# Retention in small steps inside the attention, block-diagonal states, and VectorE sums in the norm and the down tail

## The chip, the cores and the metric

One Trainium2 chip, one of its cores. The metric is the device time of one execution in microseconds (us), the median over runs. A profiled execution of the same kernel gives the trace. TensorE is PE in the rows (PEld is its weight load), VectorE is DVE, ScalarE is ACT, GpSimd is POOL, SyncE is SP.

## The reference, cut to what matters

Two layers of a trunk over 9 tiles of 128 tokens: tiles 0 to 7 are latent tokens, tile 8 is context. Each layer is

```python
h = rmsnorm(x, norm[0]) * (1.0 + sc1) + sh1
x = x + g1 * rmsnorm(mixer(h), norm[1])      # retention, Fourier, attention, Hyena; one output projection
h = rmsnorm(x, norm[2]) * (1.0 + sc2) + sh2
f = (silu(h @ w_gate) * (h @ w_up)) @ w_down
x = x + g2 * rmsnorm(f, norm[3])
```

The retention has 4 heads of 64, chunks of 128 tokens, and runs forward and backward:

```python
scores = einsum(qc, kc) * dmask              # within a chunk
inner = einsum(scores, vc)
kv = einsum(kc * zeta, vc)                   # a chunk's own 64x64 state
S_next = g_chunk * S + kv_j                  # scan over chunks
cross = einsum(qc * xi, S_prev)
o = inner + cross                            # then a norm over each head, and a gate
```

Beside it stands softmax attention with 4 heads over 9 blocks of keys for the latent tiles.

## The kernel before, in words

All of it is float32. A large product splits each operand into two float32r parts and takes three matmuls (`mm3`, L129 to L131); small products are plain float32, which the trace shows as two passes for each matmul. A scheduler puts each engine's instructions into an order from the order of the source, priorities and its own estimate of durations; at run time each engine follows its order and waits where it must. All layers run one after the other in five stages.

- `phase1`: the first norm, the input projection (`acc`), the Hyena filters and convolution. In layer 0 `norm_mod` (L306) makes each tile `x0`: a VectorE multiply (L313), a sum (L157, helper `tt`) on the engine its argument names, GpSimd by default, then `norm_turn` (L318), eight transposes into `pstr` (L324) and a split into `Th` and `Tl`.
- `phase2`: Fourier, retention and attention. `ret_rope` rotates q and k on VectorE, `ret_tables` makes the decay tables, `ret_states` makes each chunk's state (`rkz` on VectorE, `pskv` on PE at L1062, copies into `Sall`) and scans it with a multiply into `rst` and a sum (VectorE). These three stand ahead of the attention, with a raised priority. `attention` works through 20 pairs of head and query tiles: scores `sc`, softmax, transposes of the probabilities (`pstr`, L918 and L923), products `po`. After each pair it calls `beside`, which takes one step of the retention: a whole `ret_tile` or one part of `ret_group`, 15 steps in all. `ret_tile` transposes q and k (L1088), makes the scores from 64-row halves (L1100), then for each head `inner` from `rsT` (L1107) and two cross products, 64 rows by 64 columns, from `rqx` and `Sall` (L1110).
- `phase3`: the output projection (`wo`) and the second norm. `gate_up`: the SwiGLU products (`gu`).
- `ffn`: the down product into `dq`, three groups of three tiles. `finish` (L1517) ends a tile: its norm, x + y, the next layer's norm through `norm_mod`, and in layer 0 the eight transposes of the tile (`y4`) into `Th`. The two sums of a tile are on GpSimd for tiles up to `ET` (7 in layer 0; in layer 1, which has one sum only, up to 1), otherwise on VectorE.

Of the kernel before, what the change touches and what calls it, by code (L numbers as in the profile page):

```python
# [99 lines left out]
class Kern:  # L100
# [549 lines left out]
    def phase1(self, l):  # L650
        nc, tc, A = self.nc, self.tc, self.A
        with ExitStack() as c:
# [7 lines left out]
            if l == 0:  # L660
# [285 lines left out]
    def attention(self, l, pool, hd, psp, beside):  # L946
# [6 lines left out]
        for n in range(len(pairs) + 2):  # L953
# [24 lines left out]
    def ret_tables(self, l, pool, Sall):  # L978
# [33 lines left out]
        scratch = Sall[:, 4:8].rearrange("p t a b c -> p (t a b c)").rearrange("p (n c) -> p n c", c=P)  # L1012
# [15 lines left out]
    def ret_rope(self, l, keep):  # L1028

        nc = self.nc  # L1030
        tabs = keep.tile([P, 2, 8, 64], F32, name="ropeR")
        nc.sync.dma_start(tabs, self.A["ropeR"])
        Sall = keep.tile([P, 8, 2, 2, 64], F32, name="Sall")
        self.qk = keep.tile([P, NT, 512], F32, name="rqk")
        for t in range(NT):
            if t % 3 == 0:
                nc.sync.dma_start(self.qk[:, t:t + 3], self.proj[l][:, t:t + 3, 256:768])
            if t < CTX:
                tmp = Sall[:, 2 * (t % 2):2 * (t % 2) + 2].rearrange("p a b c d -> p (a b c) d")
                self.rope("v", self.qk[:, t].rearrange("p (h d) -> p h d", h=8), tabs[:, :, t], tmp, 8, 64)  # L1040
        return Sall

    def ret_states(self, l, zt, gt, Sall, keep, psp):

        nc, A = self.nc, self.A
        kvc = keep.tile([P, 2, 2, 64], F32, name="kvc")
        kzs = keep.tile([P, 2, 2, 4, 64], F32, name="rkz", tag="ropeR")
        for d in range(2):
            nc.sync.dma_start(Sall[:, 7 * d, :, d], A["sret"][l, :, :, d])
        for t in range(NT):  # L1050
            if t % 3 == 0:
                v3 = keep.tile([P, 3, 256], F32, name="rv")
                nc.sync.dma_start(v3, self.proj[l][:, t:t + 3, 768:1024])
# [10 lines left out]
            for hh in range(2):  # L1064
                q = slice(64 * hh, 64 * hh + 64)
                if t == CTX:
                    nc.scalar.activation(kvc[q], ps[q, :, :, q], AF.Copy)
                    continue
                for d, dst in ((0, t + 1), (1, t - 1)):
                    if 0 <= dst < 8:  # L1070
                        nc.scalar.activation(Sall[q, dst, :, d], ps[q, :, d, q], AF.Copy)

        nc.sync.dma_start(A["o_st"][l], kvc)
        for d, order in ((0, range(1, 8)), (1, range(6, -1, -1))):
            for t in order:
                prev = t - 1 if d == 0 else t + 1
                tmp = keep.tile([P, 2, 64], F32, name="rst")
                self.tt("v", tmp, Sall[:, prev, :, d], gt[:, :, d:d + 1].broadcast_to([P, 2, 64]), ALU.mult)
                self.tt("v", Sall[:, t, :, d], Sall[:, t, :, d], tmp, ALU.add)

    def ret_tile(self, l, t, vg, o, Dm, xi, Sall, pool, psp):
# [7 lines left out]
        qkT = pool.tile([P, 4, P], F32, name="rqkT")  # L1089
# [12 lines left out]
        for e in range(2):  # L1102
            q = slice(64 * e, 64 * e + 64)
            pi = psp.tile([P, 2, 64], F32, name="psr", tag="r")
            for pr in range(2):
                h = 2 * pr + e
                nc.tensor.matmul(pi[:, pr], sT[:, h], vg[:, 64 * h:64 * h + 64], start=True, stop=not lat)  # L1107
                if lat:
                    for d in range(2):
                        nc.tensor.matmul(pi[:, pr], qx[q, pr, d], Sall[q, t, pr, d], start=False, stop=d == 1)  # L1110
            nc.scalar.activation(o[:, e::2], pi, AF.Copy)

    def ret_group(self, l, g, Dm, xi, Sall, pool, psp):

        nc = self.nc
        vg = pool.tile([P, 3, 512], F32, name="rvg")
        o = pool.tile([P, 12, 64], F32, name="ro", bufs=1)
        for j in range(3):
            self.ret_tile(l, 3 * g + j, vg[:, j], o[:, 4 * j:4 * j + 4], Dm, xi, Sall, pool, psp)
            yield  # L1120
# [19 lines left out]
        for j in range(3):  # L1140
# [3 lines left out]
            rt = pool.tile([P, 2, P], F32, name="rot", bufs=4)  # L1144
# [61 lines left out]
    def phase2(self, l):  # L1206
        nc, tc, A = self.nc, self.tc, self.A
        with ExitStack() as c:
# [11 lines left out]
            steps = (0 for g in range(3) for _ in self.ret_group(l, g, Dm, xi, Sall, rp, psp))  # L1220
# [252 lines left out]
    ET = (7, 1)  # L1473

    def ffn(self, l):
        nc, tc, A = self.nc, self.tc, self.A
        last = l == L - 1
        with ExitStack() as c:
# [38 lines left out]
            def finish(t, ps):  # L1517
# [6 lines left out]
                e = "v" if t > self.ET[l] else "g"  # L1524
                cut = [slice(512 * h, 512 * h + 512) for h in range(2)] if last and t > 6 else [slice(0, D)]
                for q in cut:
                    self.stt(y[:, q], ps[:, q], r[:, 0:1], rows[0][:, q], ALU.mult, ALU.mult)
                    self.tt(e, x[:, q], x[:, q], y[:, q], ALU.add)
                    nc.sync.dma_start(self.xd[l + 1][t][:, q], x[:, q])
                if not last:  # L1530
# [3 lines left out]
                    self.norm_mod(t, x, y, rows[1], rows[2], dn, "tr", None, e)  # L1534
                if t + 3 < NT:
                    load_x(t + 3)

            if not last:
# [7 lines left out]
            for g in range(3):  # L1546
                ps = [dn.tile([P, D], F32, name="dq", tag=f"q{j}") for j in range(3)]
                for f0, n in self.BLOCKS:
                    for j in range(3):
# [4 lines left out]
                        for f in range(f0, f0 + n):  # L1554
                            wh_, wl_, hh, hl = W[NF * g + f]
                            q = slice(j * P, j * P + P)
                            for hs in (slice(0, 512), slice(512, 1024)):
                                self.mm3(ps[j][:, hs], hh[:, q], hl[:, q], wh_[:, hs], wl_[:, hs], f == 0, f == NF - 1)
                        if f0 + n == NF:
                            finish(3 * g + j, ps[j])  # L1560
                    if g == 0 and f0 == 9:
                        load_rows(0)
                        for t in range(3):
                            load_x(t)

# [127 lines left out]
```

## Time and profile before

| | us |
|---|---|
| three runs | 3442.18, 3446.04, 3451.61 |
| median | 3446.04 |
| profiled execution, its own time | 3440.22 |
| its span in the trace | 3438.4 |
| layer 0: attention with retention | about 587 to 833 |
| layer 1: attention with retention | about 2283 to 2520 |
| layer 0: down product | about 1509 to 1813 |

The span is the time from the first to the last instruction. The trace has for each engine when an instruction ran and what it waited for, and for TensorE the granted clock: 1.00 is 2.4 GHz, and a stretch at 0.90 had a fifth of its time at 1.2 GHz. A busy PE is not PE at its peak, since matmuls overlap and their ends are modelled; how far apart matmuls start tells what they cost.

### The profile page before, as it was taken

The page shows a single profiled execution, that of the slowest core. Times are in us where ns is not written, and L with a number is a line of the kernel's source. Part 1 is how long each engine was busy: PE and PEld are TensorE (multiplying, and loading weights), DVE is VectorE, ACT ScalarE, POOL GpSimd, SP SyncE. Part 2 cuts the span into 40 slices and gives each one's busy share as a digit, 9 for nine tenths or more (in the row PEclk, how much of TensorE's full clock was granted, in tenths as well). Part 3 has the DMA queues.
Part 4 walks back from the last instruction along what each step waited for, and adds up shares of the span by engine and source line. Part 5 has one row for each costly group of instructions (what it writes and reads, how often), then busy time and mean ns, then how long its engine had stood idle before and what let it go on. Part 6 is the DMA issues. An engine that isn't in the chain of part 4 may idle for free.

```text
span 3438.4 us, 52711 instructions
## 1 busy us (share of the span) xinstructions
PE 3178.2 (92%) x19198; PEld 2827.2 (82%) x19198; DVE 2361.8 (69%) x4784; ACT 1321.3 (38%) x2510; POOL 665.6 (19%) x611
## 2 busy tenths in 40 slices
PE   7899888999979999989998999899997999998998
PEld 5768777888779999977777788798886999998887
DVE  6676887767788888855547638676767866665454
ACT  3223213555644444433333232254557322223332
POOL 2111110000055555511111011100101422220000
PEclk8899999889999999999999999998898999999999
DMA  6454555114334343365544444541052322225564
GB/s 215 127 170 133 155 163 183 45 28 136 136 93 126 114 128 111 104 203 173 186 151 138 136 132 149 163 117 34 23 162 99 100 72 77 77 65 174 182 206 137
DMA packets 350995, 440.48 MB, mean 128 GB/s; under 512 B 71530, under 2 KB 281703, under 8 KB 350224
## 3 DMA queue, kind: packets, MB, share of 16 engines
q1 hardware_dynamic: 288960, 380.15, 35.6%
q10 hardware_dynamic: 61776, 56.97, 5.4%
q8 instruction: 151, 2.47, 0.3%
q14 instruction: 108, 0.88, 0.1%
HBM read 345.01 MB, written 92.00 MB: 127 GB/s over the span
## 4 chain that ended last, share of the span: by engine, by line
PE 39%; DVE 8%; DMA 3%; ACT 3%; issue 3%; POOL 1%; SPq 0%; ACTq 0%; DVEq 0%; POOLq 0%
PE dq L129 4%; PE dq L131 4%; PE dq L130 4%; PE gu L131 4%; PE gu L129 4%; PE gu L130 4%; PE acc L131 2%; PE acc L130 2%; PE acc L129 2%; DMA wn<-in_win 1%; DVE rq_w L146 1%; PE psr L1110 1%; PE pstr L918 1%; DVE dw L125 1%; ACT y L302 1%
## 5 line engine op out<-in xcount | busy, mean ns | idle before, releaser
L129 PE MATMUL dq<-dw 128*128 128x512 f32 x792 | 312.9, 395 | 13.0 <-ACT dw L120 10.0
L130 PE MATMUL dq<-dw 128*128 128x512 f32 x792 | 312.4, 394 | 0.0
L131 PE MATMUL dq<-dw 128*128 128x512 f32 x792 | 311.0, 394 | 0.2 <-DVE dw L125 0.2
L129 PE MATMUL gu<-X,fw 128*128 128x256 f32 x1024 | 286.0, 282 | 3.7 <-DVE u L157 1.7
L160 DVE SCALAR_TENSOR_TENSOR adacc<-adw,csilu,adacc 128x256 f32<-128x256 f32 x392 | 231.9, 617 | 80.0 <-DMA adw<-in_wada 78.0
L131 PE MATMUL gu<-X,fw 128*128 128x256 f32 x1024 | 283.0, 279 | 3.6 <-DVE fw L125 3.6
L130 PE MATMUL gu<-X,fw 128*128 128x256 f32 x1024 | 282.9, 279 | 0.0
L130 PE MATMUL acc<-wlo,Th 128*128 128x256 f32 (+1 forms) x720 | 213.7, 297 | 6.5 <-DVE wlo L125 6.3
L125 DVE TENSOR_TENSOR dw<-dhr,dw 128x384 fp32r<-128x384 f32 x132 | 74.6, 569 | 208.9 <-ACT dw L120 208.8
L129 PE MATMUL acc<-whi,Th 128*128 128x256 f32 (+1 forms) x720 | 215.4, 301 | 2.2 <-ACT whi L120 1.5
L131 PE MATMUL acc<-whi,Tl 128*128 128x256 f32 (+1 forms) x720 | 215.0, 299 | 0.0
L129 PEld LDWEIGHTS gu<-X,fw 128*128 128x128 f32 x1024 | 192.7, 189 | 14.8 <-issue 7.0
L131 PEld LDWEIGHTS gu<-X,fw 128*128 128x128 f32 x1024 | 192.5, 189 | 4.0 <-DVE fw L125 4.0
L130 PEld LDWEIGHTS gu<-X,fw 128*128 128x128 f32 x1024 | 192.9, 189 | 0.0
L129 PEld LDWEIGHTS dq<-dw 128*128 128x128 f32 x792 | 151.1, 191 | 46.9 <-ACT dw L120 11.1
L129 PE MATMUL gu<-x1s,fw 128*128 128x320 f32 x576 | 180.2, 313 | 6.4 <-DVE u L157 6.4
L157 POOL TENSOR_TENSOR adacc<-adacc,adp 128x256 f32<-128x256 f32 x168 | 152.0, 905 | 157.6 <-ACT adp L272 153.9
L125 DVE TENSOR_TENSOR dw<-dwr,dw 128x1024 fp32r<-128x1024 f32 x132 | 161.4, 1225 | 29.8 <-ACT dw L120 29.4
L131 PE MATMUL gu<-x1s,fw 128*128 128x320 f32 x576 | 180.5, 313 | 1.2 <-DVE fw L125 1.2
L130 PE MATMUL gu<-x1s,fw 128*128 128x320 f32 x576 | 179.8, 312 | 0.0
L131 PEld LDWEIGHTS dq<-dw 128*128 128x128 f32 x792 | 150.9, 191 | 32.9 <-DVE dw L125 1.3
L130 PEld LDWEIGHTS dq<-dw 128*128 128x128 f32 x792 | 151.1, 191 | 31.3
(495 smaller groups left out, 9344.5 us busy)
## 6 DMA issues: line engine op xcount, KB each, us to landing
dwr<-in_wf SPq DMA_DIRECT2D x132, 512.0 KB
adw<-in_wada SPq DMA_DIRECT2D x320, 128.0 KB
dhr<-h SPq DMA_DIRECT2D x132, 192.0 KB
h<-U SPq DMA_DIRECT2D x176, 128.0 KB
X<-in_wf SPq DMA_DIRECT2D x42, 512.0 KB
fr<-in_wf SPq DMA_DIRECT2D x40, 512.0 KB
pj<-pst ACTq DMA_DIRECT2D x90, 128.0 KB
G<-gt SPq DMA_DIRECT2D x36, 256.0 KB
```

The source lines that it names most:

```text
L125: (nc.vector if elo == "dve" else nc.gpsimd).tensor_tensor(out=lo, in0=src, in1=hi, op=ALU.subtract)
L129: mm(ps, lh, rh, start=start, stop=False)
L130: mm(ps, lh, rl, start=False, stop=False)
L131: mm(ps, ll, rh, start=False, stop=stop)
L146: nc.vector.scalar_tensor_tensor(out=w, in0=a, scalar=a[:, 0:1], in1=v, op0=ALU.mult, op1=ALU.mult)
L157: (self.nc.vector if e == "v" else self.nc.gpsimd).tensor_tensor(out=out, in0=a, in1=b, op=op)
L160: self.nc.vector.scalar_tensor_tensor(out=out, in0=a, scalar=s, in1=b, op0=op0, op1=op1)
L302: nc.scalar.activation(junk, x, AF.Square, accum_out=ss)
L918: T(pst[:, j], pr[i][:, (k0 + j) * P:(k0 + j + 1) * P], self.ident)
L1110: nc.tensor.matmul(pi[:, pr], qx[q, pr, d], Sall[q, t, pr, d], start=False, stop=d == 1)
```

## The change

Four things change.

- **Norm.** In layer 0 the nine sums of the first norm go from GpSimd to VectorE.
- **Down tail.** All sums of `finish` go to VectorE. In layer 0 the transposes of a finished tile are no longer issued in `finish`, but later: when two tiles are pending, or in the next group at its second block.
- **States.** `Sall` holds for each pair of heads a 128x128 block with the two 64x64 states on its diagonal and zeros beside them (two GpSimd memsets). A latent tile's cross products are then four matmuls of 128 rows by 128 columns, where there were eight of 64 by 64. The scan is one VectorE instruction for each pair of heads (`stt`, 128x128), two for each step, where it was a multiply and a sum.
- **Weaving.** `ret_states` and `ret_group` become one generator, `retention`, with a pause after each chunk's state, each direction of the scan and each third of a `ret_tile`: 44 steps. `beside` is also called between scores and transposes, up to 64 times. `ret_rope` and `ret_tables` stay where they were; the rotation's scratch moves out of `Sall`. Some tiles share buffers: `rv` with `rvg`, `kvc` with `rqkT`; `rot` has two buffers in place of four.

```diff
-                    self.norm_mod(t, xt[t], xt[t], rw[:, 0], rw[:, 1], psp, "tr", rs[t])
+                    self.norm_mod(t, xt[t], xt[t], rw[:, 0], rw[:, 1], psp, "tr", rs[t], "v")
...
                     probs[n].append(self.att_scores(score[i], ops[h], pool, psp))
+                beside(n)
                 if i < len(turn):
...
+        for hh in range(2):
+            nc.gpsimd.memset(Sall[64 * hh:64 * hh + 64, :, :, :, 64 - 64 * hh:P - 64 * hh], 0.0)
...
-                        nc.scalar.activation(Sall[q, dst, :, d], ps[q, :, d, q], AF.Copy)
+                        nc.scalar.activation(Sall[q, dst, :, d, q], ps[q, :, d, q], AF.Copy)
+            yield
...
-                tmp = keep.tile([P, 2, 64], F32, name="rst")
-                self.tt("v", tmp, Sall[:, prev, :, d], gt[:, :, d:d + 1].broadcast_to([P, 2, 64]), ALU.mult)
-                self.tt("v", Sall[:, t, :, d], Sall[:, t, :, d], tmp, ALU.add)
+                for k in range(2):
+                    self.stt(Sall[:, t, k, d], Sall[:, prev, k, d], gt[:, k, d:d + 1], Sall[:, t, k, d], ALU.mult, ALU.add)
+            yield
+
+    def retention(self, l, tabs, Sall, keep, pool, psp):
+
+        zt, gt, Dm, xi = tabs
+        yield from self.ret_states(l, zt, gt, Sall, keep, pool, psp)
+        for g in range(3):
+            yield from self.ret_group(l, g, Dm, xi, Sall, pool, psp)
...
-        for e in range(2):
-            q = slice(64 * e, 64 * e + 64)
-            pi = psp.tile([P, 2, 64], F32, name="psr", tag="r")
-            for pr in range(2):
-                h = 2 * pr + e
-                nc.tensor.matmul(pi[:, pr], sT[:, h], vg[:, 64 * h:64 * h + 64], start=True, stop=not lat)
-                if lat:
-                    for d in range(2):
-                        nc.tensor.matmul(pi[:, pr], qx[q, pr, d], Sall[q, t, pr, d], start=False, stop=d == 1)
-            nc.scalar.activation(o[:, e::2], pi, AF.Copy)
+        yield
+
+        pi = psp.tile([P, 4, 64], F32, name="psr", tag="r")
+        for pr in range(2):
+            both = pi[:, 2 * pr:2 * pr + 2].rearrange("p h e -> p (h e)")
+            if lat:
+                nc.tensor.matmul(both, qx[:, pr, 0], Sall[:, t, pr, 0], start=True, stop=False)
+            for h in (2 * pr, 2 * pr + 1):
+                nc.tensor.matmul(pi[:, h], sT[:, h], vg[:, 64 * h:64 * h + 64], start=not lat, stop=not lat)
+            if lat:
+                nc.tensor.matmul(both, qx[:, pr, 1], Sall[:, t, pr, 1], start=False, stop=True)
+        nc.scalar.activation(o, pi, AF.Copy)
+        yield
...
-            rt = pool.tile([P, 2, P], F32, name="rot", bufs=4)
+            rt = pool.tile([P, 2, P], F32, name="rot")
...
-                zt, gt, Dm, xi = self.ret_tables(l, rk, Sall)
-                self.ret_states(l, zt, gt, Sall, rk, psp)
+                tabs = self.ret_tables(l, rk, Sall)
...
-                e = "v" if t > self.ET[l] else "g"
...
-                    self.tt(e, x[:, q], x[:, q], y[:, q], ALU.add)
+                    self.tt("v", x[:, q], x[:, q], y[:, q], ALU.add)
...
-                    self.norm_mod(t, x, y, rows[1], rows[2], dn, "tr", None, e)
+                    self.norm_mod(t, x, y, rows[1], rows[2], None, None, None, "v")
+                    late.append((t, y))
...
+                        if len(late) > 1 or late and f0 == 3:
+                            self.norm_turn(*late.pop(0), dn, "tr")
                         if f0 + n == NF:
                             finish(3 * g + j, ps[j])
```

What the scheduler makes of it on TensorE at two places.

The first is the down product of layer 0, at the end of its first group. `dq_16282` before and `dq_16224` after are the third tile's sums, `dq_17014` and `dq_16928` the first sums of the next group, `y4_16796` and `y4_16738` the first tile's finished rows. Before:

```order
L130 MATMUL dq_16282<-dw_16758 128x512
L324 MATMUL pstr_16832<-ident_66,y4_16796 128x128 x4
L324 MATMUL pstr_16839<-ident_66,y4_16796 128x128 x4
L131 MATMUL dq_16282<-dw_16758 128x512
L129 MATMUL dq_17014<-dw_16767 128x512
```

After:

```order
L131 MATMUL dq_16224<-dw_16700 128x512
L129 MATMUL dq_16928<-dw_16709 128x512
...
L129 MATMUL dq_16928<-dw_16780 128x512
L324 MATMUL pstr_16878<-ident_66,y4_16738 128x128 x4
L324 MATMUL pstr_16885<-ident_66,y4_16738 128x128 x4
```

From the end of the first tile to its transposes there were 47 matmuls of 512 columns, and there are 55.

The second is a latent tile of the retention inside the attention of layer 0, its last third (`psr`), with the scores (`sc`) and transposes (`pstr`) of the attention around it. Before:

```order
L918 MATMUL pstr_6066<-ident_66,pr_5904 128x128 x4
L1107 MATMUL psr_6022<-rvg_6001,rsT_6013 128x64
L1110 MATMUL psr_6022<-Sall_5435,rqx_6011 128x64 x2
...
L935 MATMUL po_6111<-pth_5901,vhl_5740 128x256
...
L1110 MATMUL psr_6030<-Sall_5435,rqx_6011 128x64 x2
L129 MATMUL sc_6075<-at_Tl0_5697,at_Th0_5696 128x384
```

After:

```order
L1114 MATMUL psr_6278<-rqkT_6245 128x128 x2
L129 MATMUL sc_6289<-at_Tl1_5765,at_Th1_5764 128x384
...
L131 MATMUL sc_6299<-at_Tl1_5765,at_Th1_5764 128x384
L1122 MATMUL psr_6306<-Sall_5473,rqx_6247 128x128
L1124 MATMUL psr_6306<-rvg_6118,rsT_6276 128x64 x2
L1126 MATMUL psr_6306<-Sall_5473,rqx_6247 128x128
...
L918 MATMUL pstr_6316<-ident_66,pr_6188 128x128 x4
```

Twelve matmuls have become eight, no 64-row matmul stands among them, and nine score matmuls stand between the tile's second third (L1114) and its last.

## Rows read from the trace of the kernel before

**Rows 1.** The page: its span.
```profile
span 3438.4 us, 52711 instructions
```

**Rows 2.** Stretches: length, busy PE, PEld, DVE, ACT, POOL; granted clock, DMA share, GB/s.
```profile
625.00:795.00 170.00, 162.24 (x1041) 144.82 (x1040) 116.01 (x340) 88.97 (x181) 17.55 (x13) 0.90 0.13 34
795.00:833.00 38.00, 32.01 (x225) 28.34 (x224) 34.76 (x89) 26.75 (x49) 1.47 (x1) 1.00 0.47 155
2310.00:2500.00 190.00, 179.61 (x1143) 161.84 (x1142) 130.78 (x387) 99.11 (x200) 19.00 (x14) 0.88 0.15 41
1589.00:1650.00 61.00, 52.80 (x221) 42.63 (x220) 39.52 (x86) 23.77 (x38) 16.90 (x6) 0.89 0.57 184
1695.00:1756.00 61.00, 51.40 (x223) 41.55 (x222) 39.33 (x86) 23.67 (x38) 16.79 (x6) 0.94 0.58 189
1801.00:1850.00 49.00, 42.27 (x225) 35.51 (x224) 35.07 (x79) 14.81 (x32) 10.24 (x4) 0.93 0.55 171
```

**Rows 3.** Timeline of PE over the last third of one latent retention tile.
```profile
635.83 0.43 PE L1107 MATMUL psr<-rvg,rsT 128*128 128x64 f32 x2
636.20 0.66 PE L1110 MATMUL psr<-Sall,rqx 64*128 64x64 f32 x4
...
637.73 0.39 PE L935 MATMUL po<-pth,vhl 128*128 128x256 f32 x1
637.96 0.33 PE L1107 MATMUL psr<-rvg,rsT 128*128 128x64 f32 x2
...
639.75 0.47 PE L129 MATMUL sc<-at_Tl,at_Th 96*128 96x384 f32 x1
```

**Rows 4.** Instructions of L1110 and L1100, and a run of full-height passes on PE.
```profile
L1110 PE MATMUL psr<-Sall,rqx x256: 272/272/473, 636.2 to 2465.9; 64*128 64x64 f32 x128
2295.81 2.02 PE L1062 MATMUL pskv<-rv,rkz 128*128 128x128 f32 x16
631.01 0.72 PE L1100 MATMUL psr<-rqkT 64*128 64x128 f32 x8
```

**Rows 5.** Waits of PE from 590 to 830: total us, times, longest.
```profile
PE pskv L1062 <- DMA rv<-pj: 4.4, 2, 3.8
```

**Rows 6.** Waits of PE from 1580 to 1860.
```profile
PE pstr L324 <- POOL y L157: 20.4, 7, 4.5
```

**Rows 7.** Timelines of POOL and VectorE in and behind that tail.
```profile
1601.36 3.27 POOL L157 TENSOR_TENSOR y<-y,r 128x1024 f32<-128x1024 f32 x1 [4.91 <-issue]
1602.35 2.30 DVE L146 SCALAR_TENSOR_TENSOR rq_w<-rq_u,ss 128x1 f32<-128x1 f32 x1
1607.93 0.21 DVE L146 SCALAR_TENSOR_TENSOR rq_w<-rs,ss 128x1 f32<-128x1 f32 x1
1832.59 1.22 DVE L157 TENSOR_TENSOR x<-x,y 128x1024 f32<-128x1024 f32 x1
```

**Rows 8.** Waits of PE from 40 to 180, and VectorE's timeline there.
```profile
PE pstr L324 <- POOL x0a L157: 4.3, 2, 3.8
PE pstr L324 <- POOL x0c L157: 4.1, 2, 2.2
PE pstr L324 <- POOL x0b L157: 3.0, 2, 1.6
53.69 2.90 DVE L125 TENSOR_TENSOR wlo<-wraw,whi 128x576 fp32r<-128x576 f32 x1
58.74 0.74 DVE L125 TENSOR_TENSOR wlo<-wraw,whi 128x576 fp32r<-128x576 f32 x1
```

**Rows 9.** VectorE's work for the states, both layers: ns least, median, most.
```profile
L157 DVE TENSOR_TENSOR rkz<-rqk,rzt x36: 407/421/442, 589.6 to 2304.4; 128x256 f32<-128x256 f32 x36
L157 DVE TENSOR_TENSOR rst<-Sall,rgt x28: 273/282/1149, 589.4 to 2319.4; 128x128 f32<-128x128 f32 x28
L157 DVE TENSOR_TENSOR Sall<-Sall,rst x28: 272/281/293, 594.2 to 2319.9; 128x128 f32<-128x128 f32 x28
```

**Rows 10.** The chain that ended last: the landing of a 128 KB transfer like `rot`'s.
```profile
2199.39 3.05 DMA mixH<-hyt
```

More of the change, by code (lines that the diff above doesn't have):

```diff
@@ L1011, in ret_tables @@
         nc.scalar.activation(gt, lt, AF.Exp, scale=float(P))
-        scratch = Sall[:, 4:8].rearrange("p t a b c -> p (t a b c)").rearrange("p (n c) -> p n c", c=P)
+        scratch = Sall[:, 4:6].rearrange("p t a b c -> p (t a b) c")
         dist, tm, prow = scratch[:, 0:4], scratch[:, 4:6], scratch[:, 6:8]
@@ L1032, in ret_rope @@
         nc.sync.dma_start(tabs, self.A["ropeR"])
-        Sall = keep.tile([P, 8, 2, 2, 64], F32, name="Sall")
         self.qk = keep.tile([P, NT, 512], F32, name="rqk")
+        part = [keep.tile([P, 8, 64], F32, name="rtmp", tag=tg) for tg in ("rD", "rxi")]
         for t in range(NT):
@@ L1038, in ret_rope, with ret_states @@
             if t < CTX:
[L1039 to L1043, printed above, removed]
+                self.rope("v", self.qk[:, t].rearrange("p (h d) -> p h d", h=8), tabs[:, :, t], part[t % 2], 8, 64)
+        return keep.tile([P, 8, 2, 2, P], F32, name="Sall")
+    def ret_states(self, l, zt, gt, Sall, keep, pool, psp):
         nc, A = self.nc, self.A
-        kvc = keep.tile([P, 2, 2, 64], F32, name="kvc")
+        kvc = pool.tile([P, 4, P], F32, name="kvc", tag="rqkT")[:, 0:2].rearrange("p a (b e) -> p a b e", b=2)
         kzs = keep.tile([P, 2, 2, 4, 64], F32, name="rkz", tag="ropeR")
+        for hh in range(2):
+            nc.gpsimd.memset(Sall[64 * hh:64 * hh + 64, :, :, :, 64 - 64 * hh:P - 64 * hh], 0.0)
         for d in range(2):
-            nc.sync.dma_start(Sall[:, 7 * d, :, d], A["sret"][l, :, :, d])
+            for hh in range(2):
+                q = slice(64 * hh, 64 * hh + 64)
+                nc.sync.dma_start(Sall[q, 7 * d, :, d, q], A["sret"][l, q, :, d])
         for t in range(NT):
             if t % 3 == 0:
-                v3 = keep.tile([P, 3, 256], F32, name="rv")
+                v3 = pool.tile([P, 3, 512], F32, name="rv", tag="rvg")[:, :, 0:256]
                 nc.sync.dma_start(v3, self.proj[l][:, t:t + 3, 768:1024])
@@ L1088, in ret_tile @@
             nc.tensor.transpose(ps[:, j], self.qk[:, t, j * P:j * P + P], self.ident)
-        qkT = pool.tile([P, 4, P], F32, name="rqkT")
+        qkT = pool.tile([P, 4, P], F32, name="rqkT", tag="rqkT")
         nc.scalar.activation(qkT, ps, AF.Copy)
@@ L1101, in ret_tile @@
             nc.vector.tensor_tensor(out=sT[:, e::2], in0=pe[e], in1=Dm[:, e::2], op=ALU.mult)
[L1102 to L1111 removed]
+        yield
[9 more added lines that the diff above has]
+        nc.scalar.activation(o, pi, AF.Copy)
+        yield
     def ret_group(self, l, g, Dm, xi, Sall, pool, psp):
         nc = self.nc
[L1116 removed]
+        vg = pool.tile([P, 3, 512], F32, name="rvg", tag="rvg")
         o = pool.tile([P, 12, 64], F32, name="ro", bufs=1)
         for j in range(3):
[L1119 to L1120 removed]
+            yield from self.ret_tile(l, 3 * g + j, vg[:, j], o[:, 4 * j:4 * j + 4], Dm, xi, Sall, pool, psp)
         st = self.sm.tile([P, 12], F32, name="rmu")
@@ L1215, in phase2 @@
                 Sall = self.ret_rope(l, rk)
-                zt, gt, Dm, xi = self.ret_tables(l, rk, Sall)
-                self.ret_states(l, zt, gt, Sall, rk, psp)
+                tabs = self.ret_tables(l, rk, Sall)
             at = c.enter_context(tc.tile_pool(name="at", bufs=2, reuse_waits="tile", side="right"))
             hd = c.enter_context(tc.tile_pool(name="hd", bufs=1, reuse_waits="tile", side="right"))
-            steps = (0 for g in range(3) for _ in self.ret_group(l, g, Dm, xi, Sall, rp, psp))
+            steps = self.retention(l, tabs, Sall, rk, rp, psp)
             self.attention(l, at, hd, psp, lambda n: next(steps, None))
@@ L1533, in finish @@
                             getattr(self, f"T{nm}")[t // 3] = self.tp.tile([P, 8, 384], F32R, name=f"T{nm}{t // 3}")
-                    self.norm_mod(t, x, y, rows[1], rows[2], dn, "tr", None, e)
+                    self.norm_mod(t, x, y, rows[1], rows[2], None, None, None, "v")
+                    late.append((t, y))
                 if t + 3 < NT:
                     load_x(t + 3)
+            late = []
             if not last:
@@ L1564, in ffn @@
                             load_x(t)
+            for x in late:
+                self.norm_turn(*x, dn, "tr")
     def run(self):
```

1 line of the change is left out of this document (removed).

## The prediction

> **What bounds the kernel now.** I read the page first, then the stretches with their granted clock, then who waits for whom in the places that the diff touches, then the timelines there. The span is 3438.4 us [rows 1]; the execution took 3440.22, which is 5.8 below the median of the runs, so the sum below is made against 3440.2 and a measured median may lie a few us above its result. TensorE is the engine that the others feed. In the attention with retention it is busy for 162.24 of 170 us in layer 0 and 179.61 of 190 in layer 1, while VectorE has 116.01 and 130.78 [rows 2]: there the reader is to see an engine without room, so what leaves its queue shortens the stretch. The same rows show the second thing, the granted clock: 0.90 and 0.88 in these two stretches, where retention tiles stand between the attention's matmuls, and 1.00 in the 38 us behind them, where the attention is alone. At 0.90 the lost tenth of 170 us is 17 us; at 0.88 it is 22.8 us of 190. In the down tail of layer 0 and in its first norm TensorE does wait, and for GpSimd: 20.4 us in 7 waits for `y` [rows 6], and 4.3, 4.1 and 3.0 us for the tiles `x0` [rows 8].
>
> **The change part by part.**
>
> *States merged.* A latent tile's last third ran from 635.83 to 639.75, with one foreign `po` from 637.73 to 637.96 in it, so 3.92 - 0.23 = 3.69 us [rows 3]. In it are 8 passes of L1107 and 16 of L1110: the profile counts 256 of L1110 for 16 latent tiles [rows 4]. Four passes of L1110 take 0.66 us to the end of the last. The new third has 4 matmuls of 128x64 and 4 of 128x128, 16 passes, all on the full height. Sixteen full-height passes with 128 columns took 2.02 us [rows 4]. That saves 1.67 us for a tile, 26.7 us for 16. It is TensorE's own time in a stretch where TensorE has no room, so I take all of it; the zero halves cost nothing more, since the 2.02 us is for 128 columns already. Bounds: 20 us if a quarter of it was cover for late operands, 30 if passes at the lower clock are spared too.
>
> The Trainium skill, page "TensorE: Matmul & The Clock Gate", Part 3 on packing small matmuls, speaks against this: matmuls that use less than the full height and lie in different row groups of the array run side by side. The trace agrees for L1100, where eight 64-row passes took 0.72 us [rows 4], but not for L1110, whose neighbours use the same half and took 0.66 us for four [rows 3].
>
> *Scan and states.* The scan was 28 multiplies and 28 sums at 0.282 and 0.281 us, both layers; it becomes 56 instructions on the same 128x128, the nearest price being these rows, so nothing changes there. The 36 `rkz` at 0.421 us stay [rows 9]. What moves is their place: with `pskv` they stood ahead of the attention in layer 0, and TensorE waited 4.4 us there for the loads `rv` [rows 5]. Woven in, attention stands between them; I take 4 us. The price if this cover is gone is VectorE's time: (36 x 0.421 + 56 x 0.28) = 31 us for both layers, as a bound on the loss. The four loads of `sret` for two, each half as high, are issued on SyncE ahead of `rv`, when nothing waits. The memsets clear 2048 elements twice on 64 partitions; GpSimd's sum of 1024 took 3.27 us [rows 7], so at most some 6.5 us each, 13 us for a layer, on an engine that is busy for 17.55 of 170 us [rows 2]; I take nothing, and the bound upwards is that VectorE is held up for as long.
>
> *Weaving.* Each third of a tile now has attention between its steps, so that the copy of `rqkT` on ScalarE or the mask on VectorE is done when TensorE comes back. The order shows nine score matmuls there. The stretches give the room: 17 + 22.8 = 39.8 us of lost clock, which rows tie to the stretches that hold retention tiles, though not all of that is retention. I take half, 20 us, bounds nothing and 40.
>
> *`rot` with two buffers.* ScalarE's third copy of a group waits until the first transfer has landed. A transfer of this size took 3.05 us [rows 10]; some 2 us of other copies and issues stand between. I take 1 us for each of six groups as a loss, 6 us, bounds nothing and 12. Behind that copy wait the softmax's exponentials, and behind these the transposes.
>
> *Down tail.* Each latent tile has two sums on GpSimd at up to 3.27 us; on VectorE one took 1.22 [rows 7]. While GpSimd held its sum, a 128x1 instruction of VectorE took 2.30 us where it otherwise takes 0.21 [rows 7]. So the chain of a tile becomes shorter by 2 x (3.27 - 1.22) = 4.1 us and by the 2.1 us of one or two such hold-ups, and the order puts 55 in place of 47 matmuls before the transposes. The longest wait was 4.5 us [rows 6], so nearly all 20.4 us go; tile 6, behind which no down product follows, keeps some. I take 17. The three stretches ran at 0.89, 0.94 and 0.93 [rows 2], which is 6.7 + 3.7 + 3.4 = 13.8 us of lost clock; with the waits gone I take half, 7 us, bounds nothing and 13.8. What is late next: VectorE, which gets two sums of 1.22 us for each tile. It was busy for 39.52 of 61 us there [rows 2] with the hold-ups in it. In layer 1 two sums leave GpSimd; nothing of TensorE waits for them: nothing.
>
> *First norm.* The three waits are 11.4 us [rows 8]. But VectorE is busy there nearly without a break, and gets nine sums of 1.22 us, 11 us; what it gets back are hold-ups such as a split of 2.90 us where the next took 0.74 [rows 8]. Chains get shorter, throughput hardly. I take 5 us, bounds a loss of 10 and a gain of 11.4.
>
> **The sum.** 26.7 + 4 + 20 - 6 + 17 + 7 + 5 = 73.7 us. 3440.2 - 73.7 = 3366.5, say **3366 us**.
>
> **The rivals.**
>
> 1. *The clock does not come back.* The dips may belong to the attention itself with its many transposes. For it: layer 1 has the lower clock with the same work. Against it: 1.00 where the attention is alone [rows 2]. The 20 + 7 us fall away: 3366 + 27 = 3393.
> 2. *The attention's own chain bounds.* With retention cheaper, TensorE may wait for ScalarE and VectorE: in the 38 us with attention alone VectorE is busy for 34.76 and TensorE for 32.01 [rows 2]. Against it: that stretch also prepares the next weights. Half of 26.7 + 4 + 20 is lost: 3366 + 25 = 3391.
> 3. *VectorE becomes the bound wherever work was put on it* (slower). In the attention the 31 us of `rkz` and scan come out from their cover and count in full, and the gains of merging, states and clock vanish behind them; in the norm the nine sums are 10 us of loss. It decides once VectorE has under a tenth of its time free, as in those 38 us. Only the tail's 24 us stay: 3440.2 - 24 + 31 + 10 = 3457. Against it: 116.01 of 170 and 130.78 of 190 leave 54 and 59 us [rows 2].
> 4. *Merging saves no passes.* If half-height passes overlapped, 26.7 us would not be there, 3366 + 27 = 3393. The 0.66 us for four of them [rows 3] speaks against it. This is what the packing rule of the page "TensorE: Matmul & The Clock Gate" in the Trainium skill would make of it.
>
> **How the numbers follow.** My forecast has 0.57, rival 1 has 0.24, rival 2 0.10, rival 3 0.06, rival 4 0.03. The predicted time is the forecast's. Downwards the range takes in the whole lost clock (+20 and +7 us) and the norm's 11.4: 3366 - 33 = 3333, and with the upper bound of merging and no loss by `rot` 3324; I set 3325. Upwards it takes in rivals 1, 2 and 4 with the full price of `rot` and half the bound of the memsets: 3393 + 6 + 13 = 3412, set to 3415. Rival 3 stays outside. Changes of under 0.3%, about 10 us, can't be told from none. Rival 3's 3457 lies past that bound on the slow side, and with smaller prices within it: slower 0.04. All other cases are faster by more, but for 0.03 in which prices add up against me: faster 0.93, same 0.03.
>
> **What would show it.** Right: L1110's 64-row passes gone, and a tile's last third at about 2 us; a granted clock of 0.94 or more over the attention with retention, and both stretches shorter by 20 to 35 us; no wait of `pstr` for GpSimd in the tail, and its stretches at 0.95 or more. Wrong: TensorE waiting in the attention for `pr`, `pl` or `ptl` of VectorE in sum for more than 20 us, VectorE busy for nine tenths there, or new waits of the first `acc` products for `wlo` in the norm. The prediction as a whole is wrong if the attention with retention still takes 225 us or more in both layers.

## The result, and the profile after

The changed kernel takes 3422.32 us (median of 4 runs, 3419.45 to 3426.29) against 3448.18 us for the kernel before, measured beside it: a ratio of 0.992, with a 95% interval from 0.9896 to 0.9945. That is faster by 26 us. The forecast was 74 us less, and its range ended at 3415 us, so the time lies outside it. Two thirds of the expected gain are missing, and the question is where they went.

The span on the changed kernel's page, which answers to [rows 1]:

```profile
span 3417.7 us, 52431 instructions
```

Its stretches, with the columns of [rows 2]. The first four rows are the attention with retention of the two layers, each cut in two; the last two are the down tail of layer 0.

```profile
617.00:657.00 40.00, 22.70 (x137) 20.04 (x136) 37.78 (x125) 19.26 (x40) 0.00 (x0) 0.79 0.53 161
660.00:826.00 166.00, 153.73 (x1127) 142.30 (x1125) 136.91 (x415) 105.69 (x220) 22.93 (x16) 0.97 0.22 67
2276.00:2318.00 42.00, 23.82 (x139) 20.40 (x137) 37.29 (x124) 17.50 (x39) 0.00 (x0) 0.76 0.43 135
2320.00:2487.00 167.00, 155.18 (x1131) 142.45 (x1130) 137.84 (x419) 106.35 (x222) 22.91 (x16) 0.97 0.22 67
1616.00:1677.00 61.00, 60.43 (x277) 49.65 (x278) 41.77 (x77) 24.68 (x38) 0.00 (x0) 1.00 0.70 226
1780.00:1830.00 50.00, 44.71 (x237) 38.19 (x236) 32.05 (x81) 16.46 (x33) 0.00 (x0) 0.97 0.52 171
```

Three things are to be seen. The bulk of each attention now runs at 0.97, where [rows 2] had 0.90 and 0.88, so the clock did come back. The tail runs at 1.00, where it had 0.89 and 0.93. But at the head of each attention there is something new: 40 us in which TensorE is busy for 23, and VectorE for 38.

The timeline of TensorE over one latent tile's last third, which [rows 3] showed at 3.69 us, now reads:

```profile
695.60 0.39 PE L1122 MATMUL psr<-Sall,rqx 128*128 128x128 f32 x2
695.82 0.56 PE L1124 MATMUL psr<-rvg,rsT 128*128 128x64 f32 x4
696.21 0.44 PE L1126 MATMUL psr<-Sall,rqx 128*128 128x128 f32 x2
...
697.10 0.44 PE L1126 MATMUL psr<-Sall,rqx 128*128 128x128 f32 x2
```

That is 697.54 - 695.60 = 1.94 us, as forecast ("about 2 us"). So the merged states do what they should. The waits at the head of the attention (total us, times, longest): TensorE's in layer 0 and in layer 1, and SyncE's queue in layer 0:

```profile
PE pstr L918 <- DVE rt L992: 15.1, 1, 15.1
...
PE pstr L918 <- DVE rt L992: 16.6, 1, 16.6
...
SPq L1033 <- DMA pj<-pst: 23.9, 2, 13.0
```

(`rt` is a small instruction of the decay tables, which VectorE ends right behind the first split `pl`.) VectorE's timeline in layer 0 tells what it does meanwhile:

```profile
617.66 0.56 DVE L904 TENSOR_SCALAR_CACHE_REDUCE pr<-sc 128x384 f32<-128x384 f32 x1 [7.41 <-PE sc L131]
...
625.62 1.09 DVE L157 TENSOR_TENSOR rtmp<-rqk,ropeR 128x256 f32<-128x256 f32 x3
...
640.15 0.70 DVE L157 TENSOR_TENSOR rqk<-rqk,rtmp 128x512 f32<-128x512 f32 x1
...
640.89 0.69 DVE L125 TENSOR_TENSOR pl<-pstr,ph 128x512 fp32r<-128x512 f32 x1
```

The rotation of q and k for the retention stands behind the first scores (L904), and the first split of probabilities (`pl`) stands behind the rotation. Before the change the rotation ran beside the Fourier stage:

```profile
L157 DVE TENSOR_TENSOR rqk<-rqk,ropeR x8: 674/682/702, 564.4 to 580.9; 128x512 f32<-128x512 f32 x8
```

The change left the lines of the rotation where they were. What moved it is a size. `rot` has two buffers of 1 KB for each partition where it had four, and lies in the pool `rp`; the pool `rk`, which follows, therefore begins 2 KB lower. In phase 1 that place belongs to the staging tiles `pst`, and the last of the three ends 1 KB above the new beginning of `rk`. So `rk`'s first load (`ropeR`, L1033) has to wait until the last `pst` of the projection has been stored, which is what SyncE's row says: the load is issued at 619.3 us, where it was issued at 555.1 before.

One more thing differs, ahead of all this: in layer 0 the first state products of the low-rank keys (`mss`) begin at 167 us where they began at 138, and the Hyena stage's last products (`psf`) end at 550.6 us where they ended at 527.6. The norm itself is no shorter. Its waits, which replace the three of [rows 8]:

```profile
PE pstr L324 <- DVE rq_w L149: 3.8, 1, 3.8
PE pstr L324 <- DVE x0c L157: 3.0, 1, 3.0
PE pstr L324 <- DVE Tl L125: 2.9, 2, 1.8
PE pstr L324 <- DVE x0b L157: 1.6, 1, 1.6
```

The tail's 20.4 us of waits for GpSimd [rows 6] are 2.1 us for VectorE in five waits:

```profile
PE pstr L324 <- DVE y L157: 2.1, 5, 0.7
```

### The profile page after: what moved, and what is told of

Read it like the earlier page. It is cut to its first block, busy times and chain, and to the rows that moved or that the text cites. A ratio compares the mean times of both kernels' runs of the same rounds, so it can differ in the third digit from the quotient of the medians.

```text
span 3417.7 us, 52431 instructions
## 1 busy us (share of the span) xinstructions
PE 3126.6 (91%) x19070; PEld 2787.0 (82%) x19070; DVE 2359.4 (69%) x4811; ACT 1320.4 (39%) x2492; POOL 589.7 (17%) x588
## 4 chain that ended last, share of the span: by engine, by line
PE 55%; DVE 20%; DMA 12%; issue 5%; ACT 5%; POOL 2%; SPq 1%; DVEq 0%; ACTq 0%; POOLq 0%
PE gu L129 7%; PE gu L131 6%; PE gu L130 6%; DMA adw<-in_wada 6%; PE dq L131 5%; PE dq L129 5%; PE dq L130 5%; DVE adacc L160 3%; PE acc L131 2%; PE acc L129 2%; PE acc L130 2%; PE pstr L918 1%; DMA wn<-in_win 1%; PE po L935 1%; DVE gsum L404 1%
```

## The experiments

Each run is set against the kernel before as measured beside it (3448 to 3458 us); "less" and "more" below are against that. An interval of a ratio is about 0.25% wide to each side, 8 us, so a difference of two runs is good to some 10 us.

| run | us | ratio to before | interval | us less |
|---|---|---|---|---|
| changed kernel | 3422.32 | 0.992 | 0.9896 to 0.9945 | 26 |
| e1_xi | 3384.30 | 0.9797 | 0.9772 to 0.9822 | 67 |
| e2_norm_back | 3405.85 | 0.9863 | 0.9833 to 0.9893 | 46 |
| e3_xi_norm_back | 3358.75 | 0.9732 | 0.9699 to 0.9764 | 93 |
| e4_norm_alone | 3482.48 | 1.0078 | 1.0056 to 1.0101 | -31 |
| e5_one_sum | 3379.45 | 0.9775 | 0.9755 to 0.9795 | 79 |
| e6_tail_alone | 3422.57 | 0.9896 | 0.9877 to 0.9916 | 35 |
| e7_no_merge | 3412.38 | 0.9866 | 0.9847 to 0.9885 | 46 |
| e8_no_weave | 3361.64 | 0.972 | 0.9702 to 0.9738 | 96 |
| e9_full_height | 3369.97 | 0.9776 | 0.9755 to 0.9797 | 83 |
| e10_rot3_alone | 3452.29 | 1.0003 | 0.9983 to 1.0022 | 1 |
| e11_rot2_alone | 3502.43 | 1.0149 | 1.0133 to 1.0166 | -50 |
| e12_tail_sums_alone | 3418.19 | 0.9904 | 0.9877 to 0.993 | 35 |

**The late rotation.** e1 undoes nothing of the change, and `rot` keeps its two buffers; it moves one table into the pool `rp` and gives the rotation's products one buffer in place of two, so that the pool `rk` begins where it began before.

```diff
-        xi = pool.tile([P, 2, 2, P], F32, name="rxi")
+        xi = self.rp.tile([P, 2, 2, P], F32, name="rxi", bufs=1)
...
-        part = [keep.tile([P, 8, 64], F32, name="rtmp", tag=tg) for tg in ("rD", "rxi")]
+        part = [keep.tile([P, 8, 64], F32, name="rtmp", tag=tg) for tg in ("rD", "rD")]
...
+            self.rp = rp
```

> The changed kernel with one table of 2 KB (xi, the decays by position) in the pool rp in place of the pool rk, and with one buffer for the rotation's products. The pool rk then begins 2 KB higher, where it began before the change, past the last buffer of the projection's staging tile. Theory A (late rotation): with two buffers of rot the pool rk slid 2 KB down onto a staging buffer that is in use until the projection ends; so the rotation of retention stands behind the first scores on VectorE, and TensorE waits 15.1 us in layer 0 and 16.6 us in layer 1 for its first transposes of probabilities. It expects both waits gone, the rotation under the Fourier stage again, and 25 to 32 us less: 3390 to 3398 us against 3422. Theory B (the attention's own chain bounds, as in rival 2 of the prediction): the wait is only moved, TensorE waits as long for pr, pl and ptl a little later; 3415 us or more.

Measured: 67 us less than before, 41 better than the changed kernel. The 15.1 and 16.6 us are gone from the waits, and the rotation starts at 590 us, ahead of the scores at 624:

```profile
L157 DVE TENSOR_TENSOR rqk<-rqk,ropeR x8: 678/692/694, 591.4 to 614.0; 128x512 f32<-128x512 f32 x8
L1033 SPq DMA_DIRECT2D ropeR<-in_ropeR x1: 328/328/328, 584.1 to 584.1; - x1
```

It is more than the two waits (31.7 us), and the clock can be the rest: the two heads above stand at 0.79 and 0.76, and from the first scores to the last `po` of both layers TensorE spent 68.3 us at its lower level in the changed kernel and 34.1 in e1.

Two runs take the size by itself, in the kernel before:

```diff
-            rt = pool.tile([P, 2, P], F32, name="rot", bufs=4)
+            rt = pool.tile([P, 2, P], F32, name="rot", bufs=3)
```

> The kernel before with three buffers for rot in place of four, nothing else. The pool rk begins 1 KB lower, just at the end of the last staging buffer of phase 1 and not on it. Theory A (what delays the rotation is the overlap with that staging buffer): no change, within 6 us of the kernel before. Theory B (fewer buffers for rot make ScalarE wait for a transfer, as in the prediction's step of 6 us for two): 3 to 6 us slower.

and the same with `bufs=2`:

> The kernel before with two buffers for rot in place of four, nothing else. The pool rk begins 2 KB lower, 1 KB of it on the last staging buffer of phase 1; the rotation stands behind the first scores on VectorE. Theory A (the overlap): 20 to 50 us slower than the kernel before, with a wait of 10 us or more of TensorE at the head of the attention in both layers; here the states stand behind the rotation and ahead of the retention tiles. Theory B (only the buffers count): 6 us slower by the prediction's step, 12 at its bound.

With three buffers `rk` begins just clear of the staging tile, and the time is the same (ratio 1.0003). With two it is 50 us slower. The same waits in e11, TensorE's in both layers and SyncE's in layer 0:

```profile
PE sc L129 <- DVE pr L904: 19.5, 1, 19.5
...
PE pstr L918 <- DVE rt L991: 14.7, 1, 14.7
...
SPq L1032 <- DMA pj<-pst: 14.6, 1, 14.6
```

So it is the overlap, not the number of buffers: e1 has two buffers as well, without the overlap, and without the waits. One KB on a tile that is still in use turns nothing into 50 us. Theory A stands.

**The first norm.** e2 is the changed kernel, e3 is e1, each with the nine sums on GpSimd again; e4 is the kernel before with the nine sums on VectorE alone.

```diff
-                    self.norm_mod(t, xt[t], xt[t], rw[:, 0], rw[:, 1], psp, "tr", rs[t], "v")
+                    self.norm_mod(t, xt[t], xt[t], rw[:, 0], rw[:, 1], psp, "tr", rs[t])
```

> The changed kernel with the sums of layer 0's first norm on GpSimd again. Theory A (the norm's sums move the order of phase 1): in the changed kernel the Hyena stage of layer 0 ends 21 to 23 us later than before, with the norm itself no shorter, and TensorE has 6.7 us of work in the 30 us from 200 to 230 while VectorE makes the second filter; with the sums back this goes: 3398 to 3405 us. Theory B: the late end of that stage has another cause, such as the scheduler answering to the changed code behind it; 3417 to 3430 us, the same as the changed kernel. By the prediction's own step (first norm worth 5 us) it would be 3427.

> Both edits at once: the table xi in rp, and the first norm's sums on GpSimd. If the late rotation costs 25 to 32 us and the norm's sums 17 to 24 us and they lie in different stages, both come back: 3366 to 3380 us, which is the time that the prediction named. If the first of the two only moves a wait, 3395 to 3405; if neither is the cause, 3415 to 3425.

> The kernel before, with the sums of layer 0's first norm on VectorE and nothing else. Theory A (the norm's sums cost phase 1 of layer 0): 17 to 24 us slower, 3465 to 3472 us against 3448. Theory B (not the norm): within 5 us of the kernel before. The prediction's step: 5 us faster, 3443.

Sums back on GpSimd are worth 20 us in the changed kernel (e2) and 26 behind e1 (e3); alone in the kernel before, VectorE sums cost 31 us (e4). All three agree in sign and size: the step that was to bring 5 us loses 20 to 31. And e3, with both causes taken away, is the fastest so far, 93 us below the kernel before. e1 and e3 came out below the ranges expected of them, and e4 above its own: both causes cost more than the waits alone had let expect. The expectation of e2 has TensorE at work for 6.7 us from 200 to 230 us in the changed kernel; its trace shows 16.02.

Why VectorE sums cost so much, e5 tells. It moves a single sum of the nine, and yet TensorE's order behind the norm is that of nine moved sums:

```diff
-                    self.norm_mod(t, xt[t], xt[t], rw[:, 0], rw[:, 1], psp, "tr", rs[t], "v")
+                    self.norm_mod(t, xt[t], xt[t], rw[:, 0], rw[:, 1], psp, "tr", rs[t], "v" if t == 8 else "g")
```

> The kernel of the run with xi in rp, with eight of the first norm's nine sums on GpSimd again and only the last tile's (tile 8) on VectorE. On TensorE the order of phase 1 behind the norm is then the one of nine sums on VectorE, word for word, though only one sum of 1.2 us has moved. Theory A (the order costs the time: the products of the low-rank keys stand ahead of the filter's chain on VectorE and leave TensorE without work beside it): 3378 to 3392 us, as with nine sums (3384). Theory B (VectorE's added time in the norm costs it): about 3 us over the run with all sums on GpSimd, 3358 to 3364 us.

Measured: 79 us less than before, 12 more than e1's 67, with intervals that overlap, and 14 short of e3. So one sum costs more than half of what nine cost, though it takes VectorE 1.79 us: that part is put down to the order. The 12 us between e5 and e1 may be VectorE's time, or error, and the 14 are not far from the error either. What the order does is seen in the traces. Two stretches of phase 1 (columns of [rows 2]) in the kernel before:

```profile
140.00:150.00 10.00, 10.00 (x47) 9.85 (x46) 6.57 (x13) 1.51 (x3) 0.00 (x0) 0.74 0.00 0
...
200.00:230.00 30.00, 26.67 (x151) 24.15 (x150) 27.40 (x37) 7.33 (x16) 6.79 (x1) 1.00 0.08 23
```

The same stretches in e4:

```profile
140.00:150.00 10.00, 3.98 (x9) 3.20 (x10) 10.00 (x20) 0.00 (x0) 0.00 (x0) 0.51 0.08 20
...
200.00:230.00 30.00, 13.95 (x39) 9.63 (x39) 27.59 (x38) 4.89 (x10) 6.73 (x1) 0.64 0.19 57
```

And in e5:

```profile
140.00:150.00 10.00, 3.78 (x9) 3.06 (x10) 10.00 (x20) 0.00 (x0) 0.00 (x0) 0.59 0.05 14
...
200.00:230.00 30.00, 15.27 (x45) 10.24 (x44) 28.17 (x37) 5.85 (x12) 6.73 (x1) 0.67 0.24 72
```

In both stretches VectorE makes a Hyena filter (a reduction, a reciprocal, `gy`), a chain of its own. Before, TensorE has 47 and 151 matmuls beside it. In the other order those products have been issued earlier, 9 and about 40 are left, and TensorE waits 9.2 us (e4) and 9.3 us (e5) in one piece for `gy` (2.5 before) and loses the clock as well.

**Merging, height and weaving.** e7 takes e3 and puts a latent tile's last third back as it was, woven as now:

```diff
-            both = pi[:, 2 * pr:2 * pr + 2].rearrange("p h e -> p (h e)")
...
+                    for d in range(2):
+                        nc.tensor.matmul(pi[:, pr], qx[q, pr, d], Sall[q, t, pr, d, q], start=False, stop=d == 1)
+            nc.scalar.activation(o[:, e::2], pi, AF.Copy)
```

> The fastest kernel so far (xi in rp, first norm's sums on GpSimd, 3359 us) with a latent tile's last third as it was before: sums and 64-row state products by half, 8 passes of one and 16 of the other, in two tiles with a copy for each half. The states stay padded and the weaving stays. The prediction's step says 26.7 us (bounds 20 and 30) for 16 tiles: 3379 to 3389 us. Rival 4 (half-height passes run beside each other): 3359 us, the same. If TensorE has room there after all: 3359 to 3368.

e8 takes e3 and undoes the weaving: the states ahead of the attention, a tile in one step, `beside` once for each pair of head and query tiles.

```diff
-                beside(n)
                 if i < len(turn):
...
-        yield
...
+            with tc.high_priority(offset=100):
+                for _ in range(NT + 14):
+                    next(steps)
```

> The fastest kernel so far (3359 us) with the merged last third, but not woven: the states ahead of the attention as before the change, a tile of retention in one step, and one step for each head. The prediction's steps for weaving and state waits say 20 + 4 us (bounds 0 and 44): 3383 us, with a granted clock of 0.90 or less again in the attention with retention. Rival 1 (the clock dips belong to the attention itself): 3359 to 3363 us, with the clock the same as in the woven kernel.

Merging is worth 93 - 46 = 47 us, far over its bound of 30; weaving is worth nothing (e8 is 3 us faster, inside the error). So the clock does not come back through the weaving. e9 asks whether it is the height of the matmuls. It is e7 with one line changed, so that the 64-row products run over 128 rows, with zeros in the other half; their number stays:

```diff
-                        nc.tensor.matmul(pi[:, pr], qx[q, pr, d], Sall[q, t, pr, d, q], start=False, stop=d == 1)
+                        nc.tensor.matmul(pi[:, pr], qx[:, pr, d], Sall[:, t, pr, d, q], start=False, stop=d == 1)
```

> The kernel of the run without merging, with the same 24 passes of a latent tile's last third, in two tiles and with two copies, but each state product over all 128 rows: qx of both halves against the padded state, whose other half is zero. Only the height of 8 matmuls of a tile changes. Theory A (the half-height passes lower the granted clock: 0.86 in the attention without merging, 0.96 and 0.99 with it): the clock comes back to 0.94 or more with the same number of passes, and the time lies near the merged kernel, its 3359 us plus some 10 to 20 for the added passes: 3368 to 3385. Theory B (what counts is the number of passes and of switches between copies): 3405 to 3415 us, as without merging (3412), with the clock at 0.88 or less.

Measured: 83 us less, 37 better than e7 with the same 24 passes for a tile; the fewer passes and the one copy in place of two are then worth 93 - 83 = 10. Stretches of the two attentions in e3, merged and woven:

```profile
625.00:770.00 145.00, 134.31 (x975) 123.44 (x974) 117.36 (x362) 89.02 (x175) 19.08 (x14) 0.96 0.15 39
...
2280.00:2405.00 125.00, 117.29 (x852) 108.16 (x850) 98.14 (x300) 73.31 (x143) 19.51 (x13) 0.96 0.11 30
```

In e7, with half-height products:

```profile
625.00:770.00 145.00, 137.54 (x855) 124.11 (x853) 96.92 (x295) 73.66 (x150) 16.11 (x12) 0.86 0.14 39
...
2300.00:2455.00 155.00, 146.79 (x943) 131.29 (x941) 102.18 (x314) 77.95 (x159) 21.33 (x14) 0.90 0.09 24
```

In e8, merged and not woven, for layer 0:

```profile
625.00:770.00 145.00, 135.99 (x971) 119.08 (x970) 117.89 (x345) 92.84 (x178) 17.27 (x13) 0.99 0.24 72
```

In e9, not merged but in full height:

```profile
625.00:770.00 145.00, 135.12 (x997) 125.99 (x995) 110.46 (x339) 83.27 (x172) 17.57 (x13) 0.95 0.13 36
...
2280.00:2405.00 125.00, 117.71 (x891) 108.82 (x890) 94.36 (x286) 73.27 (x149) 17.17 (x13) 0.99 0.11 29
```

0.86 and 0.90 with half-height products, 0.95 to 0.99 without, woven or not. And the fall of the clock can be watched. TensorE's timeline in e7, over one last third, with sums (L1123) and state products (L1126) by turns:

```profile
662.11 0.33 PE L1123 MATMUL psr<-rvg,rsT 128*128 128x64 f32 x2
662.37 0.66 PE L1126 MATMUL psr<-Sall,rqx 64*128 64x64 f32 x4
662.95 0.43 PE L1123 MATMUL psr<-rvg,rsT 128*128 128x64 f32 x2
663.32 0.66 PE L1126 MATMUL psr<-Sall,rqx 64*128 64x64 f32 x4
...
664.27 0.91 PE L1126 MATMUL psr<-Sall,rqx 64*128 64x64 f32 x4
...
665.72 1.11 PE L1126 MATMUL psr<-Sall,rqx 64*128 64x64 f32 x4
```

Two stretches of e7, up to the third group of four products and behind its beginning:

```profile
659.00:664.40 5.40, 5.40 (x40) 4.82 (x39) 3.19 (x11) 1.78 (x4) 1.12 (x1) 1.00 0.06 12
664.50:667.00 2.50, 2.50 (x11) 2.15 (x11) 0.00 (x0) 0.13 (x1) 0.00 (x0) 0.51 0.02 7
```

The profile shows TensorE busy for 5.40 of 5.40 us, and no wait, when the clock drops to its lower level; after that four products take 1.11 us in place of 0.66.

e9 takes away two things at once, the half height and the changes of height, since in e7 the 64-row products stand between 128-row sums. The same place in e9:

```profile
657.25 0.33 PE L1123 MATMUL psr<-rvg,rsT 128*128 128x64 f32 x2
657.42 0.61 PE L1126 MATMUL psr<-Sall,rqx 128*128 128x64 f32 x4
657.87 0.39 PE L1123 MATMUL psr<-rvg,rsT 128*128 128x64 f32 x2
```

At the full clock a pass follows another of its own line after 112 ns, in half height as in full height (medians of L1126 in e7 and e9). But a pass of the other height follows only after 202 to 205 ns in e7, where e9 has 112 between the two lines. So half-height passes are not slower in themselves; the changes of height are most of what they cost in time. A tile's 24 passes take 3.69 us in the kernel before [rows 3] and 2.79 in e9, which is 14 us for 16 tiles. The clock is the other part: at its lower level TensorE spent 88.7 us of the two attentions in e7 and 27.3 in e9, and at half speed that is 31 us. By the traces this makes 45 us, by the runs 37.

What of the two lowers the clock, no run separates. The scores of a retention tile run over 64 rows in e3, e8 and e9 as well, eight passes in a row, and there no fall is of this kind: before each of the 17 falls of the clock in the attentions of these three, TensorE was idle for at least 1.5 of the last 4 us.

**The down tail.** e6 is the kernel before with the tail's part of the change alone, e12 with its sums on VectorE and no deferral:

```diff
-                e = "v" if t > self.ET[l] else "g"
+                e = "v"
```

> The kernel before with the down tail's part of the change alone: its sums on VectorE and the norm's transposes deferred. By the prediction's step, 17 us of waits and 7 us of clock: 24 us less, 3428 us against 3452. By the trace of the changed kernel, where layer 0's down tail is some 24 to 30 us shorter, 3422 to 3428. Rival: VectorE becomes late with the sums, so that only the waits go and others come: 3445 us or more.

> The kernel before with the down tail's sums on VectorE, and the norm's transposes where they were, not deferred. With sums and deferral it was 35 us less than before. Theory A (the sums are the gain, since each wait was for GpSimd's y and the sums on VectorE take 4.1 us less for a tile): 20 us less or more, 3430 us at most. Theory B (the deferral is the gain, since the transposes stand behind more products): 10 us less at most, 3440 us or more, with waits of the transposes for y on VectorE.

Both give 35 us. The sums are the gain; deferring the transposes adds nothing that can be measured. It spares a few us of waits: 2.1 us for `y` in e6, against 2.8 and one wait of 3.5 for `rs` in e12. The tail's first stretch in e12:

```profile
1600.00:1661.00 61.00, 60.33 (x276) 49.13 (x275) 46.62 (x98) 27.98 (x44) 0.00 (x0) 1.00 0.65 216
```

And the waits of its transposes:

```profile
PE pstr L324 <- DVE rs L150: 3.5, 1, 3.5
PE pstr L324 <- DVE y L157: 2.8, 5, 1.1
```

## Why the prediction was wrong, point by point

*Where it failed.* Two steps. The first is "`rot` with two buffers", priced at 6 us by what the buffers do on ScalarE. The run with two buffers alone shows 50 us, and three buffers none: the price is the place of the pool that follows, by which the rotation becomes late. In the changed kernel it cost 41 us (e1) to 47 (e3 against e2). No rival had it. It was within reach: the order of the changed kernel has the rotation behind the first scores on VectorE, as the timeline above shows. The step on "scan and states" weighed what moved into the attention, and not whether the rotation, whose lines had not moved, was still where it had been. The prediction's own mark for being wrong as a whole came true by this: from the first scores to the last `po` the attention takes 226 and 229 us, over its 225 (244 and 236 before, 212 and 203 in e1).

The second is "First norm", a gain of 5 us with a loss of 10 as its bound. It is a loss of 20 to 31. The view that VectorE has little room was right, and the norm's own length hardly changed: its transposes end at 92.2 us before, at 93.4 in the changed kernel and at 95.5 in e4. What was missed is that a scheduled kernel answers to a moved sum far behind it: the products that covered the Hyena filters were brought forward. The bound was worked out from VectorE's time alone.

*Where it was right by the sum and wrong by the cause.* "States merged" (26.7), "state waits" (4) and "Weaving" (20) make 51 us, and e7 and e8 put what they brought at 47 and about 0. The passes came as forecast, 3.69 to 1.94 us for a tile, 28 us for 16, but only half of this is their number: 24 passes in full height take 2.79 us, and the other half is mostly the changes of height, which the step did not have. The clock came back too: half of the lost 39.8 us was forecast, and 0.96 to 0.99 was reached. But it came with merging, not with weaving: e7, woven and not merged, stands at 0.86 and 0.90, as the kernel before did at 0.90 and 0.88. The step took the dips in the clock for the work of gaps between a tile's steps. The trace of the kernel before says otherwise for most of them, and would have said so in time. In its two attentions the clock falls 19 times, and 13 of these times at least 8 of the 64-row passes of L1110 ran just before. Before the other six TensorE had been idle for about half the time or more, as from 681.0 to 684.4 us, where it was busy for 1.27 of 3.40. One of these, in the kernel before, as two stretches:

```profile
635.80:639.90 4.10, 4.10 (x27) 3.53 (x27) 3.39 (x10) 0.98 (x4) 0.00 (x0) 1.00 0.08 16
640.00:643.40 3.40, 3.40 (x15) 3.31 (x15) 1.58 (x4) 1.78 (x4) 0.00 (x0) 0.51 0.00 0
```

The stretch from 635.80 is the tile of [rows 3], with TensorE shown busy to the last, and right behind it the clock is at its lower level. Added up over both attentions, TensorE spent 88.7 us at the lower level before and as much in e7, but 27.3, 30.7 and 23.9 in e9, e3 and e8.

*Right.* The down tail, in direction and mechanism: the waits for GpSimd are gone, and the first stretch's clock is 1.00 where it was 0.89. Its size was 35 by the runs and not 24. In the traces the way from layer 0's first down product to layer 1's first scores is 778.2 us before, 751.0 in e6 and 750.8 in e12, 27 us less; where the rest of the 35 lies is not shown. Rival 2 (the attention's own chain bounds) and rival 3 (VectorE becomes the bound wherever work was put on it) are not what happened: in the bulk of the attention the waits for `pl`, for `pr` and for `ptl` each sum to under 5 us in a layer. VectorE does bound the 40 us at the head, but with the rotation, whose place the change moved and which the rival does not name. Rival 1 (the clock does not come back) and rival 4 (merging saves no passes) fell. Rival 4 drew on the Trainium skill, page "TensorE: Matmul & The Clock Gate", Part 3, by which small matmuls of different row groups run side by side. These products follow each other in the same half, so no run here tests that rule on them; what the runs show is that half height gains these products nothing, as passes of either height start 112 ns apart, and that the kernel is 37 us faster with them in full height.

*What adds up.* Before to changed: 47 for merging, 35 for the tail, less 41 to 47 for the rotation and 20 to 31 for the norm, make 4 to 21 us of the 26 measured. That e3 is 93 below the kernel before, and merging and tail make only 82, leaves some 11 us that no run took apart, hardly more than the error. The waits for `rv` [rows 5] and the attention's waits of `po` for VectorE's `o`, 6.4 us in each layer before and 1.3 after, are candidates; this is argued, not shown.

*A version that beats both.* e3: the change with `xi` in the pool `rp` and the first norm's sums left on GpSimd, 3358.75 us, a ratio of 0.9732 (0.9699 to 0.9764) to the kernel before. e8, the same without weaving, can't be told from it.

## What to carry to other kernels

Where buffers are cut or tiles resized, look at what the pool behind them now lies on and who still uses that place: the price is not the buffer's own wait but the load that can't start. Before a dip of the clock is put down to gaps, read what TensorE ran right before it; where a few small products stand between larger ones, price the change from one shape to the other as well as the products; and where a scheduler sets the order, compare the order far behind a small edit as well as at it, above all what stands beside long chains of another engine.

## What the runs showed of the hardware

- Float32 matmuls over 64 rows between others over 128 rows went with a lower granted clock while the profile shows TensorE busy without a break: 0.86 and 0.90 with them, 0.95 and 0.99 when the same number runs over 128 rows with zeros (e7, e9). Padding with zeros was worth 37 us. Whether it is the height or the changes of height is not shown.
- A change between 64 and 128 rows took 202 to 205 ns from start to start, where passes of one height took 112, half or full (e7, e9).
- Nine sums of 1.22 us moved from GpSimd to VectorE, 11 us, made VectorE's work for the norm only some 2 us longer. What GpSimd's sums had held up became shorter by 8.9 us in sum: a split `wlo` took 2.90 us in e3 and 0.75 in e1, a small `rs` 2.33 and 0.17, like the hold-up of [rows 7] (2.30 us against 0.21).
